# A two-layer hybrid transformer backbone: the additions and multiplications of GpSimd go to VectorE

## The chip, the cores and the metric

The kernel runs on one core of one Trainium2 chip. The metric is the device time of one execution in microseconds (us), from start to end. Three runs of the kernel before took 3027.81, 3032.04 and 3037.07 us; the median is 3032.04 us. A further execution was taken by the hardware profiler and took 3032.16 us.

A core has a TensorE (PE, matrix products; PEld is its weight load), a VectorE (DVE), a ScalarE (ACT), a GpSimd (POOL) and a SyncE (SP), which issues the DMAs here. Each engine takes its own instructions strictly in the order in which they stand in its queue and waits for the others by semaphores.

## The reference

Two layers over 1024 latent tokens and 256 context tokens of width 1024, all in float32. Each layer is a token mixer followed by a SwiGLU channel mixer:

```python
h = rms_norm(x, g_norm1[l]) * (1.0 + sc1) + sh1
mix, mix_c = token_mixers(h, hc, ...)        # h @ w_in, then three groups of heads:
    # A: attention over a window of +-128 tokens and the context, QK-norm, rotary positions
    # B: real part of a 2-D DFT and a linear map
    # C: chunked gated linear attention (GLA), forward and backward
x = x + gt1 * (mix @ w_out[l])
h2 = rms_norm(x, g_norm2[l]) * (1.0 + sc2) + sh2
x = x + gt2 * swiglu(h2, w_ffn_in[l], w_ffn_out[l])   # hidden width 2816 = 22 tiles of 128
```

The scales and shifts (sc, sh, gt) come from `silu(c) @ w_mod[l] + b_mod[l]`. In the first layer the context stream goes through the same steps; the second layer only reads it.

## The kernel before, in words

All activations lie with features on the partitions and tokens along the row. Every float32 operand of a large product is split in two: `hi` is the operand rounded to the fast matmul format (ACT, line 163), `lo` is what is left (`raw - hi`, DVE, line 164). A product then takes three matmuls of 128x128 by 128x512 (lines 168 to 170). So each weight tile and each activation tile passes once through ACT and once through DVE before PE can use it.

A layer has these stages, which overlap at their ends. Times are those of the profiled execution.

- **Mixing stage** (up to about 900 us in layer 0, 1730 to 2300 us in layer 1): projections (`project`, `qk`), attention (`attend`), GLA (`gla`), the Fourier mixer, and in layer 0 the whole context FFN, woven together by a table of weights (`weave`). `qk` rotates q and k: DVE shuffles, one engine multiplies the shuffled copy by the sines (line 597), DVE multiplies the other by the cosines (598) and adds (599). `gla` masks a 256-wide block of scores in two directions with `copy_predicated` into the two halves of one buffer `abuf` (DVE, 874) and adds the two halves (876); the next block overwrites the buffer, so it waits for that addition. Line 906 multiplies the normed GLA output by the gate.
- **Output projection, norm and the first FFN tiles** (`lat_proj`, `norm_raw`, `ffn_plain`).
- **The loop of seven products** (`ffn_seven`, about 1034 to 1425 us in layer 0 with 20 of the 22 hidden tiles, about 2505 to 2755 us in layer 1 with 14). For the latent tokens the gate and up products of a hidden tile are a Strassen-Winograd scheme: instead of eight half-depth products it does seven (`p` 0 to 6), 12 matmuls each. Five of the seven weights are sums or differences of halves of the gate and up tiles (line 1222), made three products ahead of their use. The activation side needs sums and differences as well: `combos1` makes `1+` (additions) and `4-`, `3-` (subtractions, all in `combo`, line 1156), `combos2` makes `7+` and adds `r += x` in place for `6+` (line 1164). Each of these tiles is then split (163, 164). The results of the products are joined by DVE from PSUM (lines 1270 to 1286), and a PSUM bank is used again once it has been read: the first product's bank (p 0) is read by an ACT copy (1268) and used again by p 3; the second product's (p 1) is read by the DVE addition 1270 and used again by p 4. In layer 0 two modulation rows of the next layer are made per hidden tile: a DMA of one row of `wmodT` and a DVE multiply-and-reduce (328), which stands in DVE's queue and waits there for its DMA.
- **Down projection** (`down_tiles`, `down_mm`).

The order within an engine's queue is not the order of the code: the tile framework's scheduler sets it from the priorities of the code's order, its own idea of when an operand is ready, and the buffers that come free. Another engine for an instruction therefore changes the order of others too.

Of the kernel before, what the change touches and what calls it, by code (L numbers as in the profile page):

```python
# [13 lines left out]
ALU = mybir.AluOpType  # L14
# [30 lines left out]
class Prog:  # L45
# [539 lines left out]
    def qk(self, l, s, nm, j, ps, t0, n, rope):  # L585
        nc, mp = self.nc, self.mp
        raw, sq, a = self.ptmp(n, t0)
        nc.scalar.copy(raw, ps)
        nc.scalar.activation(sq, ps, ACTF.Square)
        ms = self.t_ps(n)  # L590
        nc.tensor.matmul(ms, self.onesbd[:], sq, start=True, stop=True)
        nr = self.neg_rstd(ms, 64.0, sq, a)
        g = self.nqkg[:, l, 0:1] if nm == "q" else self.nqkg[:, l, 1:2]
        nc.vector.scalar_tensor_tensor(raw, raw, g, nr, ALU.mult, ALU.mult)
        if rope is not None:
            nc.vector.stream_shuffle(sq, raw, mask=[(i + 16) % 32 for i in range(32)])
            nc.gpsimd.tensor_tensor(sq, sq, rope[:, 1, :], ALU.mult)
            nc.vector.tensor_tensor(raw, raw, rope[:, 0, :], ALU.mult)
            nc.vector.tensor_tensor(raw, raw, sq, ALU.add)
        hi, lo = sq.bitcast(F32R), raw.bitcast(F32R)  # L600
        self.split(raw, hi, lo)
        if nm == "q":
            dst = self.dram[s, "q"]
            b0, b1 = t0 // 128, (t0 + n) // 128
            for half in range(2):
                h = half * 4 + j
                for part, src in ((0, hi), (1, lo)):
                    nc.sync.dma_start(
                        dst[b0:b1, part * 64:part * 64 + 64, h, :].rearrange("b p q -> p b q"),
                        src[half * 64:half * 64 + 64, :].bitcast(F32).rearrange("p (b q) -> p b q", q=128))  # L610
        else:
            kd = self.kdl if s == "l" else self.kdc
            for kv in range(2):
                for half, src in ((0, hi), (1, lo)):
                    nc.sync.dma_start(
                        kd[half * 64:half * 64 + 64, kv, t0:t0 + n].bitcast(F32), src[kv * 64:kv * 64 + 64, :].bitcast(F32))
# [105 lines left out]
    def gla(self, l, s, need):  # L722
# [34 lines left out]
        for j in range(2):  # L757
# [99 lines left out]
            for c in range(nq):  # L857
                cs = slice(c * cw, (c + 1) * cw)
                yield from self.wait((l, s, "gr", j, (c + 1) * cw))
                ats = []  # L860
                for hh in range(2):
                    qd, en, st, _ = heads[hh]
                    tps = []
                    for d in range(2):
                        tp = self.g_ps(cw)
                        rows = slice(d * 64, d * 64 + 64)
                        for b in range(cw // 128):
                            bs = slice(c * cw + b * 128, c * cw + (b + 1) * 128)
                            nc.tensor.matmul(tp[:, b * 128:(b + 1) * 128], en[rows, bs], qd[rows, bs], start=True, stop=True)
                        tps.append(tp)  # L870
                    at = tmp("e")
                    for z in range(0, cw, 256):
                        for d in range(2):
                            nc.vector.copy_predicated(
                                self.abuf[d], self.glam[d][:].rearrange("p a b -> p (a b)"), tps[d][:, z:z + 256])
                        nc.gpsimd.tensor_tensor(at[:, z:z + 256], self.abuf[0], self.abuf[1], ALU.add)
                    ats.append(at)
                    yield 2.0
                O = self.g_ps(cw)
                for hh in range(2):  # L880
                    h = 2 * j + hh
                    qd, en, st, _ = heads[hh]
                    at = ats[hh]
                    orow = slice(hh * 64, hh * 64 + 64)
                    for b in range(cw // 128):
                        gb = c * (cw // 128) + b
                        nc.tensor.matmul(O[orow, b * 128:(b + 1) * 128], vg[:, gb, 128 + h * 64:192 + h * 64],
                                         at[:, b * 128:(b + 1) * 128], start=True, stop=False)
                        for z in range(2):
                            ch = 2 * gb + z  # L890
                            nc.tensor.matmul(O[orow, b * 128 + z * 64:b * 128 + z * 64 + 64],
                                             st[:, ch::nch], qd[:, ch * 64:(ch + 1) * 64],
                                             start=False, stop=z == 1)
                ob = tmp("b")
                sq = tmp("kt")
                nc.scalar.copy(ob, O)
                nc.scalar.activation(sq, O, ACTF.Square)
                yield 4.0
                ms = self.g_ps(cw)
                nc.tensor.matmul(ms, self.onesbd[:], sq, start=True, stop=True)  # L900
                a = tmp("e")
                nr = self.neg_rstd(ms, 64.0, sq, a)
                nc.vector.scalar_tensor_tensor(ob, ob, self.nglg[:, l:l + 1], nr, ALU.mult, ALU.mult)
                sr = tmp("e")
                nc.sync.dma_start(sr, self.dram[s, "sr"][j, :, cs])
                nc.gpsimd.tensor_tensor(ob, ob, sr, ALU.mult)
                nc.sync.dma_start(self.dram[s, "mix"][:, 6 + j, cs], ob)
                yield 0.9
        self.emitted.add((l, s + "gla"))
# [241 lines left out]
    def combo(self, name, pool, tag, parts):  # L1151
        self.B[name] = self.half(pool, tag)
        for k in range(4):
            a, b, op = parts(k)
            t = self.t(self.tp, [128, 512], F32, "nx", 3)[:]
            (self.nc.vector if "+" in name else self.nc.gpsimd).tensor_tensor(t, a, b, op)
            self.split(t, *self.B[name](k))
            yield 1

    def combos2(self):  # L1160
        r, x = self.raw0, self.raw1
        yield from self.combo("7+", self.fp, FS, lambda k: (r(k + 4), x(k + 4), ALU.add))
        for k in range(4):
            self.nc.gpsimd.tensor_tensor(r(k), r(k), x(k), ALU.add)
            yield 1
        self.B["6+"] = self.half(self.fp, FS)
        for k in range(4):
            self.split(r(k), *self.B["6+"](k))
            yield 1
# [29 lines left out]
    def ffn_seven(self, l, fs, fps):  # L1199
# [7 lines left out]
        def weights(i):  # L1207
# [11 lines left out]
                    (g2, u2, ALU.subtract), (u1, g1, ALU.subtract)][p]  # L1219
            if isinstance(pair, tuple):  # L1220
                src = self.t(self.tp, [128, 512], F32, "c1", 2)[:]
                nc.gpsimd.tensor_tensor(src, *pair)  # L1222
            else:
                src = pair
            tag = (("wh", 3), ("wl", 3), ("HC", 4))[min(self.wslot % 10 % 3 if self.wslot % 10 < 9 else 2, 2)]
# [264 lines left out]
```

## Time and profile before

| | |
|---|---|
| median of three runs | 3032.04 us |
| profiled execution | 3032.16 us |
| its span (first to last instruction) | 3030.4 us |
| PE busy | 2810.1 us (93%) |
| DVE busy | 1925.5 us (64%) |
| ACT busy | 1362.1 us (45%) |
| POOL busy | 365.6 us (12%), 266 instructions |

"Busy" is the time in which an engine had an instruction in work. Matmuls overlap at their ends, and DVE's instructions by some tens of nanoseconds, so the time that one more instruction adds is read from start to start. PEclk is the granted clock of TensorE as a share of the full one (1.00 is 2.4 GHz, 0.50 is 1.2 GHz). The mean over the profiled execution was 0.959.

### The profile page before, as it was taken

The page shows a single profiled execution, that of the slowest core. Times are in us where ns is not written, and L with a number is a line of the kernel's source. Part 1 is how long each engine was busy: PE and PEld are TensorE (multiplying, and loading weights), DVE is VectorE, ACT ScalarE, POOL GpSimd, SP SyncE. Part 2 cuts the span into 40 slices and gives each one's busy share as a digit, 9 for nine tenths or more (in the row PEclk, how much of TensorE's full clock was granted, in tenths as well). Part 3 has the DMA queues.
Part 4 walks back from the last instruction along what each step waited for, and adds up shares of the span by engine and source line. Part 5 has one row for each costly group of instructions (what it writes and reads, how often), then busy time and mean ns, then how long its engine had stood idle before and what let it go on. Part 6 is the DMA issues. An engine that isn't in the chain of part 4 may idle for free. (4 is left out here: it accounts for less than half of the span.)

```text
span 3030.4 us, 38144 instructions
## 1 busy us (share of the span) xinstructions
PE 2810.1 (93%) x14042; PEld 2248.4 (74%) x14042; DVE 1925.5 (64%) x3041; ACT 1362.1 (45%) x2476; POOL 365.6 (12%) x266
## 2 busy tenths in 40 slices
PE   6999997979989889999999898996898999999999
PEld 3577676868888677887877776664676887888887
DVE  4266677787675877777547468685675567555332
ACT  3356565565554533333324356554445454333321
POOL 0000100000000434332000000010100014331000
PEclk9999997989999999999999999996899999999999
DMA  7754452434555244444746534334244332224542
GB/s 250 257 159 132 127 156 72 144 94 138 178 185 180 84 165 134 141 135 145 257 160 214 190 112 141 114 94 139 86 127 152 125 126 94 84 84 136 201 157 94
DMA packets 198042, 436.45 MB, mean 144 GB/s; under 512 B 23712, under 2 KB 59296, under 8 KB 196832
## 3 DMA queue, kind: packets, MB, share of 16 engines
q1 hardware_dynamic: 197856, 434.03, 44.1%
q8 instruction: 110, 1.80, 0.2%
q14 instruction: 76, 0.62, 0.1%
HBM read 361.85 MB, written 69.48 MB: 142 GB/s over the span
## 5 line engine op out<-in xcount | busy, mean ns | idle before, releaser
L164 DVE TENSOR_TENSOR wl<-raw,wh 128x1024 fp32r<-128x1024 f32 (+1 forms) x310 | 377.4, 1220 | 365.2 <-ACT wh L163 345.3
L163 ACT CAST wh<-raw 128x1024 fp32r<-128x1024 f32 (+2 forms) x319 | 325.7, 1025 | 528.2 <-PE mm L169 194.6
L168 PE MATMUL mm<-H,wh 128*128 128x512 f32 x716 | 290.4, 408 | 4.1 <-ACT H L163 3.7
L170 PE MATMUL mm<-H,wl 128*128 128x512 f32 x728 | 290.7, 401 | 0.0
L169 PE MATMUL mm<-H,wh 128*128 128x512 f32 x716 | 287.9, 404 | 0.8 <-DVE H L164 0.8
L168 PE MATMUL mm<-F,wh 128*128 128x512 f32 x536 | 210.4, 392 | 6.6 <-ACT F L163 3.9
L169 PE MATMUL mm<-F,wh 128*128 128x512 f32 x536 | 210.6, 393 | 0.7 <-DVE F L164 0.7
L170 PE MATMUL mm<-F,wl 128*128 128x512 f32 x524 | 205.7, 393 | 0.5 <-DVE wl L164 0.5
L168 PE MATMUL f<-F,wh 128*128 128x512 f32 x444 | 174.0, 392 | 13.8 <-ACT GC L1268 12.3
L170 PE MATMUL f<-F,wl 128*128 128x512 f32 x456 | 177.5, 390 | 0.4 <-DVE wl L164 0.4
L169 PE MATMUL f<-F,wh 128*128 128x512 f32 x444 | 173.4, 391 | 0.0
L168 PEld LDWEIGHTS mm<-H,wh 128*128 128x128 f32 x716 | 136.3, 191 | 37.1 <-issue 5.8
L168 PE MATMUL mm<-HC,wh 128*128 128x256 f32 x544 | 160.0, 295 | 3.2 <-ACT HC L163 1.8
L170 PEld LDWEIGHTS mm<-H,wl 128*128 128x128 f32 x728 | 138.4, 190 | 30.2 <-issue 2.7
L169 PEld LDWEIGHTS mm<-H,wh 128*128 128x128 f32 x716 | 136.6, 191 | 29.8 <-issue 1.9
L169 PE MATMUL mm<-HC,wh 128*128 128x256 f32 x544 | 157.2, 290 | 0.6 <-DVE HC L411 0.3
L170 PE MATMUL mm<-HC,wl 128*128 128x256 f32 x544 | 155.4, 287 | 0.8 <-DVE wl L164 0.8
L328 DVE CUSTOM_DVE_ANT_0 na<-raw,GC 128x1024 bf16<-128x1024 f32 x64 | 90.0, 1406 | 88.9 <-DMA raw<-wmodT 84.9
L674 ACT ACTIVATE P<-S,nm 128x640 f32<-128x640 f32 (+2 forms) x144 | 104.6, 732 | 71.4 <-DVE nm L670 70.7
L168 PEld LDWEIGHTS mm<-F,wh 128*128 128x128 f32 x536 | 101.1, 189 | 30.5 <-ACT F L163 5.5
L668 DVE TENSOR_REDUCE mx<-S 128x2 f32<-128x1280 f32 (+2 forms) x68 | 95.6, 1406 | 40.9 <-PE S L663 40.4
L696 PE MATMUL t<-ident,P 128*128 128x128 f32 x640 | 110.5, 289 | 11.6 <-DVE pt L701 4.3
(592 smaller groups left out, 6989.7 us busy)
## 6 DMA issues: line engine op xcount, KB each, us to landing
raw<-wff SPq DMA_DIRECT2D x228, 512.0 KB, 3.8
raw<-wmodT SPq DMA_DIRECT2D x64, 512.0 KB, 4.1
raw<-wfm SPq DMA_DIRECT2D x52, 512.0 KB, 4.0
nx<-gd SPq DMA_DIRECT2D x88, 256.0 KB, 3.8
raw<-wout SPq DMA_DIRECT2D x40, 512.0 KB, 3.7
XC<-wff SPq DMA_DIRECT2D x34, 512.0 KB, 3.8
pt<-wmod SPq DMA_DIRECT2D x64, 256.0 KB, 4.5
qld<-q_l SPq DMA_DIRECT2D x64, 256.0 KB, 4.2
```

The source lines that it names most:

```text
L163: self.nc.scalar.copy(hi, raw)
L164: (eng or self.nc.vector).tensor_tensor(lo, raw, hi.bitcast(F32), ALU.subtract)
L168: mm(ps, wh, xh, start=start, stop=False, skip_group_check=skip)
L169: mm(ps, wh, xl, start=False, stop=False, skip_group_check=skip)
L170: mm(ps, wl, xh, start=False, stop=stop, skip_group_check=skip)
L328: self.nc.vector.tensor_tensor_reduce(out=junk[:], in0=raw, in1=cs[s][:], op0=ALU.mult, op1=ALU.add, scale=1.0, scalar=0.0, accum_out=self ...
L668: nc.vector.tensor_reduce(mx[:, :nh], st[:, c0:c0 + nh * n].rearrange("p (a n) -> p a n", n=n), axis=AX.X, op=ALU.max)
L674: nc.scalar.activation(P[:, :n], st[:, c0 + z * n:c0 + (z + 1) * n], ACTF.Exp, bias=nm[:, hh:hh + 1], accum_out=sums[:, hh:hh + 1])
L696: nc.tensor.transpose(tp[:, hh * 128:(hh + 1) * 128], P[:, c:c + 128], self.ident[:])
```

## The change

Every `tensor_tensor` that was issued on GpSimd is issued on VectorE. Nothing else is edited. POOL keeps only its memsets.

```diff
@@ qk
-            nc.gpsimd.tensor_tensor(sq, sq, rope[:, 1, :], ALU.mult)
+            nc.vector.tensor_tensor(sq, sq, rope[:, 1, :], ALU.mult)
@@ gla
-                        nc.gpsimd.tensor_tensor(at[:, z:z + 256], self.abuf[0], self.abuf[1], ALU.add)
+                        nc.vector.tensor_tensor(at[:, z:z + 256], self.abuf[0], self.abuf[1], ALU.add)
...
-                nc.gpsimd.tensor_tensor(ob, ob, sr, ALU.mult)
+                nc.vector.tensor_tensor(ob, ob, sr, ALU.mult)
@@ combo
-            (self.nc.vector if "+" in name else self.nc.gpsimd).tensor_tensor(t, a, b, op)
+            self.nc.vector.tensor_tensor(t, a, b, op)
@@ combos2
-            self.nc.gpsimd.tensor_tensor(r(k), r(k), x(k), ALU.add)
+            self.nc.vector.tensor_tensor(r(k), r(k), x(k), ALU.add)
@@ ffn_seven, weights
-                nc.gpsimd.tensor_tensor(src, *pair)
+                nc.vector.tensor_tensor(src, *pair)
```

The scheduler lays the queues out anew. Two places at the start of the loop of seven products in layer 0 show it. ACT's queue before, around the copy of the first product's bank (L1268). `nx` are the differences of activations (line 1156) and `c1` the sums of weights (line 1222), both made by POOL; `H` and `F` are split activations, `wh`, `wl` and `HC` split weights, `f` and `mm` PSUM banks:

```order
L163 CAST H_1662_9498<-nx_1666_9502 128x512
L576 ACTIVATE nx_1659_9485<-nx_1659_9485 128x512
L163 CAST wh_1704_9657<-c1_1703_9655 128x512
L163 CAST wl_1706_9682<-c1_1705_9680 128x512
L163 CAST H_1662_9498<-nx_1667_9506 128x512
L163 CAST H_1663_9499<-nx_1669_9537 128x512
L1268 COPY GC_1671_9546<-f_1681_9567 128x512
L163 CAST wh_1716_9740<-XC_1696_9626 128x512
```

The same place of ACT's queue after:

```order
L163 CAST F_1646_9433<-nx_1661_9494 128x512
L163 CAST wl_1693_9603<-raw_1673_9548 128x512
L576 ACTIVATE nx_1659_9485<-nx_1659_9485 128x512
L1268 COPY GC_1671_9546<-f_1681_9567 128x512
L163 CAST H_1662_9498<-nx_1666_9502 128x512
L163 CAST H_1662_9498<-nx_1667_9506 128x512
L163 CAST H_1663_9499<-nx_1669_9537 128x512
L163 CAST H_1663_9499<-nx_1670_9541 128x512
```

The copy L1268 has moved ahead of the casts of all four `H` tiles; before, three of them and two casts of weight sums stood ahead of it. Second place, DVE's queue before, up to the addition L1270 that frees the second product's bank:

```order
L164 TENSOR_TENSOR H_1665_9501<-nx_1669_9537,H_1663_9499 128x512
L164 TENSOR_TENSOR wl_1706_9682<-c1_1705_9680,wl_1706_9682 128x512
L1156 TENSOR_TENSOR nx_1690_9578<-XA_60_382,F_1486_8446 128x512
L164 TENSOR_TENSOR H_1665_9501<-nx_1670_9541,H_1663_9499 128x512
L1156 TENSOR_TENSOR nx_1691_9582<-XA_60_382,F_1486_8446 128x512
L164 TENSOR_TENSOR F_1688_9576<-nx_1690_9578,F_1686_9574 128x512
L1156 TENSOR_TENSOR nx_1692_9586<-XA_60_382,F_1487_8447 128x512
L164 TENSOR_TENSOR F_1688_9576<-nx_1691_9582,F_1686_9574 128x512
L1156 TENSOR_TENSOR nx_1694_9606<-XA_60_382,F_1487_8447 128x512
L164 TENSOR_TENSOR F_1689_9577<-nx_1692_9586,F_1687_9575 128x512
L1270 TENSOR_TENSOR GC_1671_9546<-GC_1671_9546,f_1682_9568 128x512
```

DVE's queue after, up to the same addition:

```order
L1164 TENSOR_TENSOR XA_60_382<-XA_60_382,F_1484_8444 128x512
L164 TENSOR_TENSOR H_1665_9501<-nx_1669_9537,H_1663_9499 128x512
L164 TENSOR_TENSOR H_1665_9501<-nx_1670_9541,H_1663_9499 128x512
L1156 TENSOR_TENSOR nx_1690_9578<-XA_60_382,F_1486_8446 128x512
L1156 TENSOR_TENSOR nx_1691_9582<-XA_60_382,F_1486_8446 128x512
L1156 TENSOR_TENSOR nx_1692_9586<-XA_60_382,F_1487_8447 128x512
L164 TENSOR_TENSOR F_1688_9576<-nx_1690_9578,F_1686_9574 128x512
L164 TENSOR_TENSOR F_1688_9576<-nx_1691_9582,F_1686_9574 128x512
L164 TENSOR_TENSOR F_1689_9577<-nx_1692_9586,F_1687_9575 128x512
L1156 TENSOR_TENSOR nx_1694_9606<-XA_60_382,F_1487_8447 128x512
L1164 TENSOR_TENSOR XA_60_382<-XA_60_382,F_1484_8444 128x512
L1270 TENSOR_TENSOR GC_1671_9546<-GC_1671_9546,f_1682_9568 128x512
```

The splits of weight sums (`wl_1706`) have moved behind L1270, and the in-place sums L1164 and the differences of `3-` and `4-` now stand ahead of it. Counted from the split of the last weight tile of the stage before (`wl_1657`), 31 instructions stand between the two in DVE's queue before, and 40 after.

## Rows read from the trace of the kernel before

**Rows 1.** Page: busy time, share of the span, instructions of each engine.

```profile
PE 2810.1 (93%) x14042; PEld 2248.4 (74%) x14042; DVE 1925.5 (64%) x3041; ACT 1362.1 (45%) x2476; POOL 365.6 (12%) x266
```

**Rows 2.** Stretches: length; busy time and instructions by engine; PEclk, DMA share, GB/s.

```profile
500.00:900.00 400.00, 365.40 (x2652) 318.17 (x2651) 301.85 (x570) 217.30 (x432) 22.10 (x20) 0.96 0.44 139
1800.00:2200.00 400.00, 335.37 (x1764) 250.97 (x1762) 285.66 (x500) 209.00 (x414) 33.83 (x29) 0.88 0.38 116
1100.00:1400.00 300.00, 293.46 (x1270) 240.03 (x1269) 238.79 (x306) 101.86 (x177) 114.89 (x80) 0.99 0.43 143
2500.00:2750.00 250.00, 245.08 (x1077) 201.62 (x1077) 147.83 (x210) 93.57 (x162) 102.80 (x70) 1.00 0.25 85
1042.00:1062.00 20.00, 5.00 (x14) 3.40 (x12) 19.73 (x19) 9.70 (x18) 13.84 (x9) 0.70 0.20 66
1062.00:1082.00 20.00, 19.46 (x77) 15.88 (x78) 15.23 (x27) 10.63 (x21) 5.47 (x3) 0.88 0.39 125
1202.00:1422.00 220.00, 219.59 (x968) 181.17 (x967) 176.00 (x226) 70.79 (x127) 78.36 (x58) 1.00 0.43 140
```

**Rows 3.** Groups of POOL: count, busy us, mean ns, idle before and its releasers.

```profile
L1222 POOL TENSOR_TENSOR c<-raw,XC 128x512 f32<-128x512 f32 x68 | 97.4, 1432 | 87.9 <-DVE HC L164 34.4 <-DVE wh L164 32.1 <-DVE wl L164 19.0
L876 POOL TENSOR_TENSOR nx<-XA 128x256 f32<-128x256 f32 x36 | 32.5, 902 | 488.8 <-DVE XA L874 282.8 <-DVE es L680 195.1 <-DVE es L678 7.0
L597 POOL TENSOR_TENSOR P<-P,XC 128x512 f32<-128x512 f32 x10 | 15.9, 1592 | 433.8 <-ACT HC L829 163.5 <-DVE P L596 148.2 <-DVE mod_0l L305 110.8
L1164 POOL TENSOR_TENSOR XA<-XA,F 128x512 f32<-128x512 f32 x8 | 11.9, 1482 | 0.5
```

**Rows 4.** Groups of DVE in the loop, 1100 to 1400 us.

```profile
L328 DVE CUSTOM_DVE_ANT_0 na<-raw,GC 128x1024 bf16<-128x1024 f32 x34 | 51.4, 1512 | 41.1 <-DMA raw<-wmodT 41.0
L1282 DVE TENSOR_TENSOR XA<-XA 128x512 f32<-128x512 f32 x15 | 21.6, 1443 | 1.6 <-ACT XA L1281 0.7
L1280 DVE TENSOR_TENSOR XA<-f,XA 128x512 f32<-128x512 f32 x8 | 5.4, 680 | 0.7 <-PE f L170 0.7
```

**Rows 5.** Groups of DVE where POOL has no arithmetic, 1450 to 1700 us.

```profile
L328 DVE CUSTOM_DVE_ANT_0 na<-raw,GC 128x1024 bf16<-128x1024 f32 x22 | 26.9, 1223 | 35.4 <-DMA raw<-wmodT 35.4
L164 DVE TENSOR_TENSOR F<-nx,F 128x512 fp32r<-128x512 f32 x38 | 25.4, 687 | 12.3 <-ACT F L163 11.9
L1282 DVE TENSOR_TENSOR XA<-XA 128x512 f32<-128x512 f32 x1 | 0.7, 684 | 0.0
```

**Rows 6.** Stretch, line 164 on DVE alone: length, busy time and count.

```profile
1100.00:1400.00 300.00, 106.52 (x110) 0.99 0.43 143
```

**Rows 7.** Order of time, DVE: start, duration, instruction, idle before it.

```profile
1022.05 1.22 DVE L164 TENSOR_TENSOR wl<-raw,wh 128x1024 fp32r<-128x1024 f32 x1
1031.47 1.78 DVE L164 TENSOR_TENSOR wl<-c,wl 128x512 fp32r<-128x512 f32 x1
1058.20 0.68 DVE L1156 TENSOR_TENSOR nx<-XA,F 128x512 f32<-128x512 f32 x1
1058.80 0.68 DVE L164 TENSOR_TENSOR F<-nx,F 128x512 fp32r<-128x512 f32 x1
1061.81 0.67 DVE L1270 TENSOR_TENSOR GC<-GC,f 128x512 f32<-128x512 f32 x1
```

**Rows 8.** Order of time, ACT, before the copy of the first product's bank.

```profile
1046.24 0.62 ACT L163 CAST H<-nx 128x512 fp32r<-128x512 f32 x1 [3.27 <-POOL nx L1156]
1052.08 0.62 ACT L163 CAST H<-nx 128x512 fp32r<-128x512 f32 x1 [1.05 <-POOL nx L1156]
1052.60 0.58 ACT L1268 COPY GC<-f 128x512 f32<-128x512 f32 x1
```

**Rows 9.** Order of time, PE: the two waits at the loop's start.

```profile
1041.97 0.39 PE L170 MATMUL f<-F,HC 128*128 128x512 f32 x1
1053.24 0.80 PE L168 MATMUL f<-F,wh 128*128 128x512 f32 x1 [10.88 <-ACT GC L1268]
1062.54 0.80 PE L168 MATMUL f<-H,wl 128*128 128x512 f32 x1 [4.66 <-DVE GC L1270]
```

**Rows 10.** Line 874 on DVE: idle before it until the named releaser, us, times.

```profile
  POOL nx L876: 6.7, 11
```

## The prediction

> **What bounds the kernel now.** I read the busy times first. PE is busy 93% of the span, DVE 64%, POOL 12% [rows 1], so only what lets PE wait can move the time, and a busier DVE costs nothing until PE waits for it. The stretches come next, because the shares differ by stage [rows 2]. In the loop of seven products PE works without a gap once it runs: 219.6 of 220 us in layer 0, 245.1 of 250 in layer 1. In the mixing stages it idles, 34.6 of 400 us at 500 to 900 and 64.6 of 400 at 1800 to 2200, with DVE at 75% and 71% and POOL nearly idle (22 and 34 us). POOL's work sits in the two loops. DVE there is busy 239 of 300 us in layer 0, and 41 us of its 61 idle us are waits of the modulation rows for their DMA [rows 4]. So layer 0's loop is where DVE has least room: some 20 us in 300.
>
> One thing in the trace says that POOL's work is not free for DVE. The same subtraction or multiplication on DVE is longer where POOL works beside it: L1282, two operands in SBUF, means 1443 ns in the loop of layer 0 and 684 where POOL has nothing to do; the modulation row takes 1512 against 1223 [rows 4, 5]; the splits of line 164 take 106.5 us for 110 in the loop, 968 each, against 687 [rows 5, 6]. L1280 has one operand in PSUM and stays at 680 [rows 4]. So an instruction of POOL holds up a DVE instruction that reads SBUF twice.
>
> The Trainium skill states it as a rule (SBUF — State Buffer, "SBUF: two separate sides"): VectorE and GpSimd share one pair of ports, and an operation of VectorE with two SBUF inputs and one of GpSimd that reads SBUF exclude each other for a whole instruction, whoever starts first. The rows above agree (1443 against 684, and 680 for the one with a PSUM input). If the two merely shared the bandwidth, some relief would come too, so the sum below does not hang on it.
>
> **What the change removes and adds.** POOL's 260 arithmetic instructions go: 170 of line 1222 (the row shown, with x68, and three like it with 34 each), 36 of L876, 20 of L597, 16 of L1156, 8 of L1164 and 10 of L906 [rows 3]. They took 900 to 1590 ns on POOL. On DVE the same subtraction L1156 is 0.68 us long, and the next instruction starts 0.60 us after it [rows 7], so I take 0.60 us for 512 columns and a little over half, 0.35, for the 38 of 256 columns.
>
> In 1100 to 1400 us DVE gets 79 additions of line 1222: 47.4 us. It is relieved of the waits for POOL: 110 x (968 - 687) = 30.9 us on line 164, 15 x (1443 - 684) = 11.4 on L1282, 34 x (1512 - 1223) = 9.8 on L328, together 52 us. So DVE's load in this stretch does not grow; it falls by about 5 us. That is the first half of the forecast: the loop stays PE's. Cost there 0; if the relief fails, see the rival below.
>
> The Trainium skill has a rule that speaks against more DVE instructions (VectorE: DVE Perf Modes, "The DRAIN you can't avoid"): after each operation the pipe empties before the next begins, so what counts is the number of operations. The trace shows starts 0.60 us apart for durations of 0.68 [rows 7], so part of that is overlapped here. By the rule an added operation would cost the whole 0.68, the load in the stretch above would be 54 us against 52 of relief, and the restart below would come 40 x 0.08 = 3.2 us later, a time of about 3023. I go by the starts.
>
> **The start of the loop in layer 0.** This is where PE pays for POOL. After the third product PE stops at 1042.0, starts p 3 at 1053.24 after 10.88 us, and after it waits 4.66 us more for p 4 [rows 9]. The first wait ends with ACT's copy L1268, which frees a PSUM bank. That copy's input, the first product, was there before the third had ended; it stood in ACT's queue behind casts that waited for POOL's differences, the last until 1052.1 [rows 8]. The second ends with DVE's L1270 at 1061.81, which stood at the end of a convoy: DVE and POOL alternated, and DVE's 512-column instructions took 1.78 us instead of 0.68 [rows 7]. 31 instructions lie between `wl<-raw,wh` (1022.05) and L1270 (1061.81): 38.6 us after the first had its 1.1 us, 1.25 each.
>
> Afterwards there are 40 between the two, with no POOL: 40 x 0.60 = 24 us, and L1270 at 1022.1 + 1.1 + 24 = 1047.2. Beside it the casts on ACT (0.62 us each [rows 8], about one for two of DVE's) keep up, and L1268 stands ahead of the four H casts in the new order. So p 3 follows at 1042.2 with no wait and ends 12 x 0.227 = 2.7 us later (0.227 = 219.59 / 968 [rows 2]), and p 4 starts at 1047.2 to 1049: a wait of 2.3 to 4. I take 4 instead of 15.5: **-11.5 us**. Bounds: -15.5 if none is left, -4 if DVE waits for ACT at every second split (the 31 instructions' average of 1.25 us would again come near).
>
> The clock: in 1042 to 1082 it was granted at 0.70 and 0.88 after the long wait, and 91 matmuls took 24.5 us [rows 2]; at 0.227 they take 20.6. That is 3.9 us, kept wholly or in part if a wait of 4 us no longer brings it down. I take half, **-2**; bounds 0 and -4.
>
> What is late next: PE arrives 13 us earlier at products whose weights DVE must still add and split, and these splits now stand behind L1270. Before, 300 - 293.5 = 6.5 us of waits followed in 1100 to 1400 [rows 2]. Each new addition also stands behind modulation rows that wait 41.1/34 = 1.2 us on average for their DMA. The cover is the lead of three products, 8 us. I add **+3**; bounds 0 and +10.
>
> **Layer 1's loop.** DVE gets 70 instructions there, 42 us on 148 of 250 [rows 2]: 76%, hidden. Of PE's 4.9 us of waits I credit **-1** (bounds -4, +3).
>
> **The mixing stages.** L597 and L598 ran side by side on paper only: both read SBUF twice, L597 took 1.59 us, and two on DVE take 1.2. L876 cost the next masking 6.7 us of waits in 11 places [rows 10], which go, for 36 x 0.35 = 13 us of work. In 500 to 900 and 1800 to 2200 the 49 instructions of POOL become some 25 us on DVE's 301.9 and 285.7 of 400 [rows 2], against relief of the same kind as above, which I put at half to all of it. Net near nothing, but the scheduler has laid out the queues of all engines anew from the first q tile on, and among 99 us of PE's waits a few may grow or go. **-1**, bounds -12 and +10.
>
> **Sum.** -11.5 - 2 + 3 - 1 - 1 = -12.5 us on the profiled 3032.16, which is the median of the runs (3032.04) to 0.1 us. Predicted: **3020 us**, its own range 3008 to 3027.
>
> **Rivals.** *Nothing that can be measured, 3030 us.* PE's earlier restart is given back within the loop: DVE stays the slower in the catch-up, where each product needs some six DVE instructions, 3.6 us, against PE's 2.7, and the waits behind the restart grow by what was saved. For it: DVE has only 20 us of true idle time in 300 there. Against it: from 1202 on PE has no waits, and DVE's load is not greater than before.
>
> *DVE becomes the bound of layer 0's loop, 3067 us.* One queue then holds the additions, the splits, the joins and the modulation rows with their DMA waits. If the relief does not come, DVE needs 238.8 + 41 + 47.4 = 327 us per 300, 9% more, over the loop's 390 us: +35 us. It decides from the point where less than 27 of the 52 us of relief arrive (238.8 + 41 + 47.4 - 27 = 300). For it: the addition of a weight, which ran on POOL while DVE waited for a modulation row, now waits behind it. Against it: the durations in rows 4 to 6 show the relief itself, instruction by instruction.
>
> *More than forecast, 3003 us.* The clock stays up at the restart, no wait is left there (-19.4), and of the 99 us of waits in the two mixing stretches a tenth (-9.9) goes with the shorter chains. For it: the waits of L874 for L876 and the slow L597 [rows 3, 10]. Against it: POOL did little there.
>
> **How the numbers follow.** The forecast has a chance of 0.47, no visible change 0.28, the DVE bound 0.13, the larger gain 0.12. A measurement of this kernel can tell about 0.3%, 9 us, from no change. Faster by more, below 3023: 0.85 of the forecast (0.40), the larger gain (0.12) and a little of the second (0.01): 0.53. Slower by more, above 3041: most of the DVE bound (0.12) and a tenth of the second case (0.03), 0.15. The rest, 0.32, is within. The range reaches from 3002, just past the larger gain, to 3046, where a part of the DVE bound is taken in.
>
> **What would show it.** After: PE's waits at L1268 and L1270 at the loop's start in layer 0 together under 6 us; DVE's 512-column instructions all near 0.68 us; L1282 near 684 and L328 near 1223 ns in the loop; DVE busy 230 to 245 of 300 us there though it holds 79 instructions more; PE at 99% from 1200 on. Wrong would be: PE waiting for line 164 or 1222 in every hidden tile of layer 0 (the DVE bound), L1282 still above 1 us without POOL, or changes of more than 10 us in the mixing stages.

## The result

The changed kernel took 2993.79 us in the median of four runs (2991.63 to 3001.51), beside 3033.78 us for the kernel before in four runs on the same chip. The medians differ by 40.0 us; the ratio is 0.9875, with a 95% interval of 0.9851 to 0.9899, which is some 38 us of the time before. The forecast was 3020 us, in a range of 3002 to 3046. The direction was right, and the gain is three times the forecast and lies outside the range.

The page's first part, after, beside [rows 1]: DVE has 260 instructions more and is busy 30 us longer, and POOL keeps six memsets.

```profile
PE 2803.1 (93%) x14042; PEld 2250.1 (75%) x14042; DVE 1955.1 (65%) x3301; ACT 1364.8 (45%) x2476; POOL 1.3 (0%) x6
```

Shares over the whole span don't show where the time went. The two loops of seven products do, cut from PE's first matmul of the loop to the start of DVE's last join. The kernel before, layer 0 and layer 1, in the columns of [rows 2]:

```profile
1034.00:1459.00 425.00, 398.38 (x1704) 324.56 (x1704) 338.24 (x434) 155.11 (x269) 154.65 (x106) 0.97 0.43 141
2514.30:2790.00 275.70, 270.78 (x1191) 222.87 (x1190) 163.59 (x234) 103.25 (x176) 96.96 (x66) 1.00 0.27 92
```

The same two after, and then the stretches of [rows 2]:

```profile
1040.60:1433.30 392.70, 388.59 (x1705) 320.62 (x1704) 326.74 (x536) 152.84 (x260) 0.00 (x0) 1.00 0.47 152
2489.80:2759.30 269.50, 269.50 (x1190) 223.23 (x1190) 192.50 (x293) 101.63 (x172) 0.00 (x0) 1.00 0.28 95
...
500.00:900.00 400.00, 362.63 (x2594) 318.33 (x2595) 295.10 (x566) 214.23 (x427) 0.00 (x0) 0.93 0.43 135
1800.00:2200.00 400.00, 337.48 (x1812) 251.05 (x1811) 284.82 (x528) 203.93 (x403) 0.00 (x0) 0.89 0.40 119
1100.00:1400.00 300.00, 300.00 (x1325) 248.47 (x1324) 247.40 (x405) 107.61 (x182) 0.00 (x0) 1.00 0.46 149
2500.00:2750.00 250.00, 250.00 (x1104) 207.07 (x1104) 174.71 (x266) 89.09 (x150) 0.00 (x0) 1.00 0.26 89
```

The same matmuls of layer 0's loop (1704 and 1705 in the records) take 392.7 us instead of 425.0 (-32.3), and those of layer 1 take 269.5 instead of 275.7 (-6.2). Together that is -38.5 us, about the whole change. From 1100 to 1400 and in all of layer 1's loop PE has no idle time left. The rest of the program did not get shorter: the part between the loops takes 1056.5 us (1055.3 before), the last stage 240.4 in both, and the part ahead of the first loop 1040.6 (1034.0 before). That last number changes from one execution to the next, also with the same kernel (further executions of the changed one began the loop at 1036.2 and 1034.7 us), and the profiled execution of 3001.51 us is the longest of the four.

At the start of layer 0's loop, after. In order of time, first DVE, then ACT, then PE (start, duration, instruction, idle before it), beside [rows 7 to 9]:

```profile
1028.56 1.22 DVE L164 TENSOR_TENSOR wl<-raw,wh 128x1024 fp32r<-128x1024 f32 x1
...
1053.78 0.67 DVE L1270 TENSOR_TENSOR GC<-GC,f 128x512 f32<-128x512 f32 x1
```

```profile
1043.47 0.59 ACT L1268 COPY GC<-f 128x512 f32<-128x512 f32 x1 [1.59 <-PE f L170]
```

```profile
1054.59 0.76 PE L168 MATMUL f<-H,wl 128*128 128x512 f32 x1 [3.00 <-ACT F L163]
```

ACT now copies the first product's bank as soon as that product is done (it waits for PE), so p 3 starts without a gap. One wait is left, 3.00 us ahead of p 4. The row names a cast of ACT, which ended at 54.50; L1270 ended at 54.45, so which of the two released it can't be told from the row. 10.88 + 4.66 us became 3.00.

DVE's groups in the loop, 1100 to 1400 us, after, beside [rows 4]:

```profile
L328 DVE CUSTOM_DVE_ANT_0 na<-raw,GC 128x1024 bf16<-128x1024 f32 x36 | 44.0, 1222 | 16.8 <-DMA raw<-wmodT 16.5
L1282 DVE TENSOR_TENSOR XA<-XA 128x512 f32<-128x512 f32 x16 | 11.0, 685 | 0.7 <-ACT XA L1281 0.7
L1280 DVE TENSOR_TENSOR XA<-f,XA 128x512 f32<-128x512 f32 x8 | 5.5, 686 | 0.7 <-PE f L170 0.7
```

Line 164 on DVE alone in the same stretch (length, busy time and count, PEclk, DMA share, GB/s), beside [rows 6]:

```profile
1100.00:1400.00 300.00, 77.41 (x114) 1.00 0.46 149
```

The three kinds of DVE instruction that were long before are now as short as in [rows 5]: L1282, L328 and line 164 take 685, 1222 and 679 ns (77.41 / 114), where they took 1443, 1512 and 968.

What the forecast had let stand shows in PE's groups behind the start, 1080 to 1440 us (mean of one, then idle before them and its releasers). Before:

```profile
L168 PE MATMUL f<-F,HC 128*128 128x512 f32 x74 | 29.5, 399 | 2.2 <-ACT HC L163 2.0 <-ACT XA L1268 0.2
...
L168 PE MATMUL mm<-F,wl 128*128 128x512 f32 x32 | 13.1, 408 | 3.6 <-ACT XA L1268 3.6
...
L168 PE MATMUL f<-H,wh 128*128 128x512 f32 x28 | 11.7, 419 | 3.1 <-DVE XA L1270 3.1
```

After, the largest wait of the same view:

```profile
L168 PE MATMUL f<-F,HC 128*128 128x512 f32 x72 | 28.1, 391 | 0.8 <-ACT HC L163 0.8
```

Before, these and smaller ones came to 11 us. After, they come to 1.1 us. The waits before were of two kinds. 5.0 us ended with a join or split of DVE (1.2 of them behind a modulation row that waited for its DMA). The longest of these, 2.1 us, shows the usual case: the join L1270 is short itself, but stood behind two splits of 1.78 and 1.74 us, where a split alone takes 0.69 [rows 5].

```profile
1187.82 1.78 DVE L164 TENSOR_TENSOR wl<-c,wl 128x512 fp32r<-128x512 f32 x1
...
1190.66 1.74 DVE L164 TENSOR_TENSOR HC<-XC,HC 128x512 fp32r<-128x512 f32 x1
1192.33 0.67 DVE L1270 TENSOR_TENSOR XA<-XA,f 128x512 f32<-128x512 f32 x1
```

The others, 5.8 us, ended with ACT. The longest wait of all, 3.6 us, is one of them: the copy L1268 stood in ACT's queue behind casts of weight sums that had not yet come from POOL. The first of the waits (2.0 us, at 1096.84) ended with the cast of a sum ahead of which POOL had itself waited for the DMA of its weights.

```profile
1124.54 0.62 ACT L163 CAST HC<-c 128x512 fp32r<-128x512 f32 x1 [3.13 <-POOL c L1222]
1126.20 0.62 ACT L163 CAST wh<-c 128x512 fp32r<-128x512 f32 x1 [1.05 <-POOL c L1222]
1126.73 0.58 ACT L1268 COPY XA<-mm 128x512 f32<-128x512 f32 x1
```

### The profile page after: what moved, and what is told of

It is laid out like the page before. It is cut to its first block, busy times and chain, and to the rows that moved or that the text cites. A ratio compares the mean times of both kernels' runs of the same rounds, so it can differ in the third digit from the quotient of the medians.

```text
span 2999.7 us, 37870 instructions
## 1 busy us (share of the span) xinstructions
PE 2803.1 (93%) x14042; PEld 2250.1 (75%) x14042; DVE 1955.1 (65%) x3301; ACT 1364.8 (45%) x2476; POOL 1.3 (0%) x6
## 4 chain that ended last, share of the span: by engine, by line
PE 71%; DVE 11%; DMA 8%; ACT 6%; issue 3%; SPq 1%; ACTq 0%; DVEq 0%
PE mm L168 11%; PE mm L169 11%; PE mm L170 11%; PE f L170 5%; PE f L168 5%; PE f L169 5%; DMA raw<-wff 3%; PE t L709 2%; PE t L696 2%; PE t L168 2%; PE t L169 2%; PE t L170 2%; DVE wl L164 2%; ACT wh L163 1%; PE S L652 1%
## 5 line engine op out<-in xcount | busy, mean ns | idle before, releaser
L168 PEld LDWEIGHTS mm<-F,wh 128*128 128x128 f32 x536 | 101.0, 188 | 31.2 <-ACT F L163 6.2
L696 PE MATMUL t<-ident,P 128*128 128x128 f32 x640 | 112.0, 292 | 12.2 <-DVE P L689 4.7
L169 PEld LDWEIGHTS mm<-F,wh 128*128 128x128 f32 x536 | 101.1, 189 | 22.7 <-DVE F L164 1.5
```

The source lines that it names most:

```text
L168: mm(ps, wh, xh, start=start, stop=False, skip_group_check=skip)
L169: mm(ps, wh, xl, start=False, stop=False, skip_group_check=skip)
L696: nc.tensor.transpose(tp[:, hh * 128:(hh + 1) * 128], P[:, c:c + 128], self.ident[:])
```

## The experiments

Two theories were open once the result was known. **Lock:** POOL's reads of SBUF stretch DVE's instructions, the joins and splits among them for which PE waits; without them all waits go. **Handoff:** what costs is that a weight sum passes from DVE's queue to POOL's and back (POOL waits for a buffer, DVE for the sum); on one engine the passing is gone. Beside them stood **order**: only the new order at the loop's start counts. "Loop" below is layer 0's, cut as above. The runs were made on several chips, on which the kernel before took 3024.5 to 3033.8 us, so each ratio is against the kernel before on the same chip, and the ranges in microseconds are to be read with that in mind.

**1. The weight sums alone on DVE**, the rest as before.

```diff
@@ ffn_seven, weights (kernel before)
-                nc.gpsimd.tensor_tensor(src, *pair)
+                nc.vector.tensor_tensor(src, *pair)
```

> Only the weight sums (line 1222, 170 of the 260 instructions) go to VectorE; the activation sums and differences stay on GpSimd. Lock theory (a GpSimd instruction that reads SBUF holds up VectorE instructions with two SBUF inputs): the steady loop of layer 0 gains (L1282 near 684 ns, L328 near 1223 from 1100 to 1400 us), the start of the loop keeps most of its convoy, so a part of the gain: 3005 to 3020 us. Order theory (the gain came from the new queue order at the loop's start, the copy L1268 ahead of the casts): near the kernel before, 3025 to 3035. Handoff theory (a weight sum on GpSimd is slow to come, and PE waits for it): most of the gain, 2995 to 3005.

3000.97 us, ratio 0.9899 [0.9883, 0.9916]. Its loop's stretch, then PE at its start in order of time:

```profile
1038.10:1438.80 400.70, 390.53 (x1704) 321.40 (x1703) 331.71 (x532) 157.21 (x268) 10.13 (x7) 0.99 0.44 149
```

```profile
1047.79 0.79 PE L170 MATMUL f<-F,HC 128*128 128x512 f32 x1 [3.61 <-DVE HC L164]
...
1053.12 0.50 PE L168 MATMUL f<-F,wh 128*128 128x512 f32 x1 [1.18 <-ACT GC L1268]
...
1060.47 0.50 PE L168 MATMUL f<-H,wl 128*128 128x512 f32 x1 [4.33 <-DVE GC L1270]
```

The time lies below the lock theory's range and inside the handoff theory's, so by the time alone this run speaks for handoff; the order theory is out. The trace is as the lock theory had it: L1282 takes 687 ns and L328 1224. The loop is 24.3 us shorter although 9.1 us of waits stay at its start. The waits at the start fall by 6.4 us, those behind it from 11.1 to 1.1, and the rest is faster matmuls: the sums bring most of the gain. One step, the sums on DVE, took away both the stretched splits and POOL's late sums, so this run can't tell the two theories apart.

**2. The activation sums alone on DVE.**

```diff
@@ combo, combos2 (kernel before)
-            (self.nc.vector if "+" in name else self.nc.gpsimd).tensor_tensor(t, a, b, op)
+            self.nc.vector.tensor_tensor(t, a, b, op)
...
-            self.nc.gpsimd.tensor_tensor(r(k), r(k), x(k), ALU.add)
+            self.nc.vector.tensor_tensor(r(k), r(k), x(k), ALU.add)
```

> Only the activation sums and differences of the loop (lines 1156 and 1164, 24 instructions) go to VectorE; the weight sums stay on GpSimd. Lock theory: the long waits at the start of layer 0's loop (15.5 us) shrink to some 6, the later ones and L1282 at 1443 ns stay: 3010 to 3022 us. Order theory: nearly the whole gain, 2995 to 3005. Handoff theory of the weight sums: 3020 to 3030.

3014.79 us, ratio 0.9943 [0.9924, 0.9961]. Its loop, a group of DVE (1100 to 1400 us), and two of PE over the loop:

```profile
1030.80:1445.20 414.40, 395.38 (x1701) 322.40 (x1700) 334.56 (x442) 151.65 (x262) 138.88 (x96) 0.98 0.43 144
```

```profile
L1282 DVE TENSOR_TENSOR XA<-XA 128x512 f32<-128x512 f32 x15 | 22.8, 1520 | 1.6 <-ACT XA L1281 0.7
```

```profile
L168 PE MATMUL f<-F,HC 128*128 128x512 f32 x84 | 33.7, 401 | 5.0 <-ACT HC L163 4.8 <-ACT XA L1268 0.2
...
L168 PE MATMUL f<-H,wh 128*128 128x512 f32 x32 | 13.4, 420 | 5.3 <-DVE XA L1270 5.3
```

The time is in the lock theory's range and outside the two others. This is the mirror image of number 1. The waits at the start fall from 15.5 to 3.3 us, L1282 stays long at 1520 ns, and the waits behind the start do not merely stay: they grow from 11.1 to 15.7 us (414.40 - 395.38 = 19.0 in the loop, less 3.3), which fits PE's earlier arrival. The loop gets 10.6 us shorter, close to what the forecast had for the restart. The two parts come to 24.3 + 10.6 = 34.9 us beside the change's 32.3, so they add up nearly. The new order at the start can explain a third of the gain at most, since this run also took POOL's differences and in-place sums away from there.

**3. The mixing stages alone on DVE** (lines 597, 876 and 906), **and the loops alone** (lines 1222, 1156 and 1164).

```diff
@@ qk, gla (kernel before; the second kernel is the changed one with these three lines put back)
-            nc.gpsimd.tensor_tensor(sq, sq, rope[:, 1, :], ALU.mult)
+            nc.vector.tensor_tensor(sq, sq, rope[:, 1, :], ALU.mult)
...
-                        nc.gpsimd.tensor_tensor(at[:, z:z + 256], self.abuf[0], self.abuf[1], ALU.add)
+                        nc.vector.tensor_tensor(at[:, z:z + 256], self.abuf[0], self.abuf[1], ALU.add)
...
-                nc.gpsimd.tensor_tensor(ob, ob, sr, ALU.mult)
+                nc.vector.tensor_tensor(ob, ob, sr, ALU.mult)
```

> Only the instructions of the mixing stages (lines 597, 876, 906, 66 of 260) go to VectorE. All theories: within 6 us of the kernel before, 3028 to 3040 us, with both loops as before; a gain of 10 us or more would say that the mixing stages had a part in it.

> The instructions of the loops (lines 1222, 1156, 1164, 194 of 260) go to VectorE; those of the mixing stages stay on GpSimd. Lock theory: the whole gain, 2990 to 3000 us. If the mixing stages had a part, 3003 or more.

The mixing stages alone: 3029.25 us, 1.0003 [0.9992, 1.0013]. The loops alone: 2990.36 us, 0.9871 [0.9855, 0.9888], with a loop of 392.7 us. Both times are in their ranges. On the chip of numbers 4, 5 and 7 the changed kernel ran once more:

> The changed kernel once more, for comparison on the same chip and for a second profile: 2990 to 3002 us. If the stages before layer 0's loop are 6 us longer than before in the first profile by chance, they are not so here; if the new order makes them so, they are.

2994.52 us, 0.9903 [0.9887, 0.992]; its layer 0 loop began at 1036.2 us, so most of the first profile's delay ahead of the loop was chance. The whole gain is the loops'; 66 instructions more or less on DVE in the mixing stages can't be told from nothing.

**4. POOL reads beside DVE, and nobody waits for it.** The changed kernel, in which POOL makes each weight sum as well (504 of its columns), into a tile `padr` that nothing reads. The line that gives this tile its name is left out of the diff here and in number 6.

```diff
@@ ffn_seven, weights (changed kernel)
                 nc.vector.tensor_tensor(src, *pair)
+                nc.gpsimd.tensor_tensor(self.padr[:], pair[0][:, 0:504], pair[1][:, 0:504], pair[2])
```

> The changed kernel with 170 idle additions on GpSimd: beside each weight sum of VectorE, GpSimd adds the same two operands (504 columns) into a pad that nobody reads. No engine waits for a result of GpSimd. Lock theory: L1282 above 1000 ns again, VectorE's load in layer 0's loop past what the loop holds, 3015 to 3050 us. Handoff theory (what cost was the way over the slow engine) and order theory: 2992 to 3002, as the changed kernel.

3066.91 us, 1.0134 [1.0119, 1.0149]: slower than the kernel before, and more than the lock theory's range had it. Its loop, two groups of DVE, and PE's waits in 1100 to 1400 us (in all, times, longest; lines 1271 and 1287 here are 1270 and 1286 before):

```profile
1036.20:1485.90 449.70, 408.40 (x1705) 328.75 (x1704) 405.74 (x546) 155.52 (x269) 146.72 (x92) 0.96 0.40 133
```

```profile
L164 DVE TENSOR_TENSOR HC<-c,HC 128x512 fp32r<-128x512 f32 x28 | 23.7, 846 | 0.0
...
L1287 DVE TENSOR_TENSOR XA<-XA 128x512 f32<-128x512 f32 x13 | 17.5, 1345 | 0.0
```

```profile
PE f L168 <- DVE XA L1271: 13.5, 5, 4.3
PE t L168 <- DVE XA L1271: 7.0, 4, 2.4
```

Nothing waits for POOL's result, and still the join of line 1286, which takes 684 ns in the changed kernel, takes 1345, DVE is busy 405.7 us of the loop instead of 326.7 for ten instructions more, and PE waits for DVE's joins. POOL does hold the weight buffers until it has read them here, which number 6 takes away. In this run DVE has the additions and the stretching together; in the kernel before it had only the stretching.

**5. POOL in the chain, and reads nothing.** The changed kernel with two memsets by POOL of the sum's tile ahead of each sum: DVE has to wait for POOL, POOL for DVE's buffer.

```diff
@@ ffn_seven, weights (changed kernel)
                 src = self.t(self.tp, [128, 512], F32, "c1", 2)[:]
+                nc.gpsimd.memset(src, 0.0)
+                nc.gpsimd.memset(src, 0.0)
                 nc.vector.tensor_tensor(src, *pair)
```

> The changed kernel with GpSimd in the chain of each weight sum and reading nothing: GpSimd writes zeros twice into the tile (0.53 us each) before VectorE overwrites it with the sum, so that VectorE waits for GpSimd as it did for the casts before. Lock theory with a lock only against instructions of GpSimd that read: VectorE's durations stay near 0.68 us, and the time within 10 us of the changed kernel, 2992 to 3004. Handoff theory: most of the gain is lost, 3015 to 3035.

2995.79 us, 0.9901 [0.9886, 0.9916], as the changed kernel and as the lock theory had it. Its loop, then a group of DVE in 1100 to 1400 us (line 1284 here is 1282 before):

```profile
1036.90:1430.20 393.30, 389.19 (x1706) 320.68 (x1706) 325.62 (x535) 152.61 (x259) 100.96 (x193) 1.00 0.46 152
```

```profile
L1284 DVE TENSOR_TENSOR XA<-XA 128x512 f32<-128x512 f32 x16 | 10.9, 684 | 0.7 <-ACT XA L1283 0.7
```

POOL is busy 101 us of the loop, is passed every tile, and costs 0.6 us. So the passing by itself costs nothing, and the handoff theory falls in that form. What this run does not have is a sum that is made on POOL: POOL can clear its tile early, and DVE waited for it only 3.0 us in 1100 to 1400. The waits for late sums on ACT, seen before, are not imitated here.

**6. POOL reads only its own tile.** As number 5 with one memset, after which POOL reads one column of the sum's tile and adds its own tile of 504 columns to itself. The own tile is cleared once when the kernel starts, in a line left out here.

```diff
@@ ffn_seven, weights (changed kernel)
                 src = self.t(self.tp, [128, 512], F32, "c1", 2)[:]
+                nc.gpsimd.memset(src, 0.0)
+                nc.gpsimd.tensor_tensor(self.padr[:, 0:1], src[:, 0:1], src[:, 0:1], ALU.add)
+                nc.gpsimd.tensor_tensor(self.padr[:], self.padr[:], self.padr[:], ALU.add)
                 nc.vector.tensor_tensor(src, *pair)
```

> The changed kernel with GpSimd reading SBUF beside the weight sums, tied to no operand of the loop: per weight sum GpSimd clears the tile (as in the run with the cleared tile, which cost nothing), reads one column of it, and then adds a pad of 504 columns to itself, a pad that no other engine touches. Unlike in the run with the idle additions, no weight buffer is held longer by it. Lock theory: VectorE's subtractions and joins with two SBUF inputs are long again, and the loop of layer 0 takes 425 to 455 us instead of 393: 3020 to 3070 us. If the idle additions cost time only because they held the weight buffers: within 8 us of the changed kernel, 2990 to 3004.

3044.45 us, 1.0055 [1.0037, 1.0072], in the lock theory's range. Its loop, groups of DVE in 1100 to 1400 us (lines 165 and 1279 are 164 and 1275 before), and what DVE waited for POOL there:

```profile
1036.40:1469.30 432.90, 399.66 (x1698) 323.28 (x1697) 370.26 (x535) 151.38 (x259) 219.60 (x291) 0.98 0.40 137
```

```profile
L165 DVE TENSOR_TENSOR wl<-c,wl 128x512 fp32r<-128x512 f32 x24 | 23.4, 974 | 0.0
...
L1279 DVE TENSOR_TENSOR XA<-XA 128x512 f32<-128x512 f32 x14 | 12.1, 864 | 0.0
```

```profile
DVE c L1226 <- POOL padr L1224: 11.7, 15, 1.7
```

No weight buffer is tied to POOL now, and the loop is 40.2 us longer than the changed kernel's; DVE is busy 370.3 us for 535 instructions, where it was 326.7 for 536. Those 43.5 us are stretched instructions. A smaller part is waiting: the sums waited 11.7 us for POOL's one-column read in 300 us. Number 4 has the stretching without any such wait, number 5 the passing without the stretching. So POOL's additions, which read SBUF, stretch DVE's instructions and cost PE time, and its memsets, which don't read, do not. That it is the read, and not something else in which an addition differs from a memset, was not tested by itself, nor why number 4 is still 17 us slower in the loop than this one.

The Trainium skill (SBUF — State Buffer, "SBUF: two separate sides") says that a VectorE operation with two SBUF inputs is blocked only by a GpSimd operation that reads SBUF. Numbers 5 and 6 agree: beside memsets the join of line 1275, with two SBUF inputs, takes 686 ns, and beside an addition of a tile that has nothing to do with it 864; the join of line 1282 rises less, from 684 to 740.

**7. A longer lead.** The kernel before, with weight sums made four products ahead instead of three.

```diff
-        ahead = 3
+        ahead = 4
```

> The kernel before with the weights of the loop made four products ahead instead of three. Handoff theory: the longer lead covers GpSimd's slow sums, and the later waits go (6.5 us in 1100 to 1400): 3015 to 3026 us. Lock theory: VectorE is held up just as much, within 6 us of the kernel before, 3027 to 3040.

3024.82 us, 0.9997 [0.9985, 1.0009]; the loop takes 425.5 us, against 425.0. The time lies in the handoff theory's range only because the kernel before, too, took no more than 3024.53 us on this chip. The later waits did not go as that theory had it (9.6 us idle in 1100 to 1400, 6.5 before). But the run decides little, because the sums hardly came earlier. The same sum of POOL, in the kernel before and here:

```profile
1109.40 1.29 POOL L1222 TENSOR_TENSOR c<-raw 128x512 f32<-128x512 f32 x1 [3.79 <-DVE mod_1c L328]
1104.92 1.28 POOL L1222 TENSOR_TENSOR c<-raw 128x512 f32<-128x512 f32 x1 [3.71 <-DVE mod_1c L328]
```

That is 75.4 and 74.3 us behind the loop's first matmul: 1.1 us earlier, less than one product of 2.7 us. What a sum that really comes earlier would be worth stays untested.

**8. The last wait at the start.** The changed kernel with two steps of the activation sums per product instead of three, which leaves 29 instead of 40 instructions ahead of L1270; then the same with the mixing stages on POOL; and the changed kernel a third time, on the same chip as the latter.

```diff
@@ ffn_seven (changed kernel)
-            for _ in range(3):
+            for _ in range(2):
                 next(sums, None)
```

> The changed kernel with two instead of three steps of the last activation sums taken per product at the start of the loop, so that 29 instead of 40 instructions stand between the last split and the addition that frees the second bank. That addition comes 11 x 0.60 = 6.6 us earlier, and the last wait of 3.0 us at the loop's start and its half-speed stretch of 3.4 us go: 2986 to 2995 us, some 4 us under the changed kernel. If the sums that are put off are then late for the sixth and seventh products, as before or slower.

> The loops' instructions on VectorE, those of the mixing stages left on GpSimd, and two steps of the activation sums per product. If the two edits that each measured some 4 us under the changed kernel are real and add up: 2985 to 2990 us and 4 to 9 us under the changed kernel run beside it. If they were scatter of the stages before the loop: within 3 us of it.

> The changed kernel beside it on the same chip: 2990 to 2998 us.

2989.7 us, 0.987 [0.9847, 0.9894]; 2986.76 us, 0.9868 [0.985, 0.9886]; and the changed kernel itself 2988.73 us, 0.9879 [0.9857, 0.9902]. The wait of 3.00 us goes, and smaller ones come in its place, as this row of PE in the first of the three shows:

```profile
1049.75 0.50 PE L168 MATMUL mm<-H,HC 128*128 128x512 f32 x1 [1.15 <-ACT HC L163]
```

The loops take 391.6, 390.0 and 392.7 us. No changed kernel ran on the chip of the first. The two edits together were 2.0 us under the changed kernel beside them, within the 3 us that had been named as scatter, and that kernel itself came out 1.3 us under its range. A gain of 1 to 3 us may be there, but the runs can't tell it from none, so none of these is a better version.

## Why the prediction was right in direction and wrong in size

Layer 0's loop lost 32.3 us. PE's idle time in it went from 425.0 - 398.4 = 26.6 us to 392.7 - 388.6 = 4.1 us, so 22.5 of the 32.3 are idle time, and the other 9.8 are matmuls that took less time, most of it a matter of the clock, as shown below.

- **The restart (-11.5): right.** The waits went from 15.5 to 3.0 us; forecast were 2.3 to 4. L1270 was put at 24 us behind the end of the last `wl` split, 40 instructions at 0.60 us from start to start: 1028.56 + 1.1 + 24 = 1053.7, measured 1053.78. By the whole durations of 0.68 it would have come 3 us later. Number 2, which changes little but the start, took 12.2 us off the waits there.
- **"What is late next" (+3): wrong, and this is the step that failed.** The term asked only what arrives late once PE comes earlier. It took the waits behind the start, 6.5 us idle in [rows 2] at 1100 to 1400, as a stock that could only grow (bounds 0 and +10), and the relief of DVE was booked as load alone: 47 us of additions against 52 us of relief, "Cost there 0". The load did stay: 238.8 us for 1270 matmuls before, 247.4 for 1325 after, 0.188 and 0.187 us each. But the waits, 11 us over the whole loop, were no matter of load. They stood behind single stretched splits and behind POOL's late sums, and both went with POOL's work: about -10 in place of +3. Number 2 shows where the step's reasoning would have held: with the weight sums still on POOL, PE's earlier arrival made these waits grow by 4.6 us. With the sums on DVE (number 1) they fell to 1.1. How the 10 us divide between the stretching and the late sums stays open, since no run has the late sums without the stretching, and the runs that stretch without them (numbers 4 and 6) load DVE with the sums besides.
- **The clock (-2): right for its stretch, but 9.8 in all.** The step looked at one stretch, 1042 to 1082, where by its count 3.9 us were lost; 1.3 are left after (25 matmuls in 7.00 us in the row below, 5.7 at 0.227). The clock also fell behind the three longest of the later waits, which the step did not price. Before, the three stretches with these waits (columns as above):

```profile
1094.00:1104.00 10.00, 7.61 (x26) 5.50 (x25) 8.32 (x10) 3.48 (x6) 5.50 (x5) 0.83 0.39 109
...
1124.00:1134.00 10.00, 6.52 (x20) 4.77 (x21) 9.05 (x9) 4.39 (x8) 5.64 (x4) 0.83 0.51 169
...
1184.00:1204.00 20.00, 17.70 (x70) 13.82 (x69) 17.17 (x22) 7.07 (x12) 10.81 (x7) 0.91 0.55 176
```

  PE idled 2.4, 3.5 and 2.3 us in them. The granted clock was 0.83 in the first two: a third of the time at the lower of its two levels, 1.2 GHz, the rest at 2.4. The 116 matmuls of the three took 31.8 us, where they take 26.3 at 0.227. The short waits at 1425 to 1430 (1.0 and 1.2 us) and those in layer 1's loop left the clock at 1.00. After, one stretch of the loop is left with less than 1.00, around the wait of 3.00 us:

```profile
1050.00:1060.00 10.00, 7.00 (x25) 5.36 (x24) 9.86 (x17) 7.22 (x13) 0.00 (x0) 0.83 0.20 55
```

  So the waits that went cost 22.5 us as idle time and up to 9.8 more in slow matmuls behind them, of which these stretches show about 8. That the slow matmuls follow the waits is read from the traces; the clock was not varied by itself.
- **Layer 1's loop (-1): too small.** It lost 6.2 us and all of its idle time (4.9 us before, of which 2.8 ended with ACT's copy L1268 and 2.2 with DVE's join L1270). Number 1 shows the same loop at 269.2 us and number 2 at 271.4, so here either half of the change takes most of the waits away; which mechanism did it was not separated.
- **The mixing stages (-1): right.** Number 3 measured 1.0003.
- **The rivals.** DVE as the bound fell with L1282 at 685 ns: all of the relief arrived. Number 4 shows what it would have looked like, with the additions on DVE and part of the relief missing: 42 us above the kernel before on its chip, where the rival had 35. That its 3066.9 us look like the 3067 worked out is chance, since the chips differ, and only 24.7 of the 42 us are in layer 0's loop, where the rival had all of its 35. "Nothing that can be measured" fell with the waits behind the start. "More than forecast", 3003 us, came nearest in time, but it looked for the rest in the mixing stages, where there was none, so that a part of its nearness is luck.
- **The signs.** Four of five came true: 3.0 us of waits at the start, the short instructions, L1282 and L328, and PE without idle time from 1200 on. DVE was busy 247.4 us of the 300, a little over the 230 to 245 named, in a stretch that now holds 55 matmuls more. One reading of the prediction was off without effect on the sum: POOL's groups took up to 1716 ns each (line 1222, `c<-XC,raw`), not 1590.

What stays open: how the gain behind the start divides between stretched DVE instructions and late sums of POOL, why number 4 is slower than number 6, and why DVE's waits of the modulation rows for their DMA fell from 41.1 us [rows 4] to 16.8 in the same stretch. The last may be no more than where the idle time is booked; no run was made for that one.

## What to carry to other kernels

Where instructions of VectorE with two SBUF operands come out longer beside GpSimd's than alone, moving GpSimd's arithmetic over may cost VectorE little, as it did here, and the gain is not the saved load but the waits of the bound engine: sum every one of them in that stage, and ask of each whether its releaser was stretched, stood behind a stretched instruction, or waited for GpSimd. Don't carry such waits over as fixed when the change removes what they wait for. Add to the longer ones what the granted clock loses behind them. Before putting work on an idle GpSimd, compare the duration of VectorE's own instructions with and without it.

## What the runs showed of the hardware that was not expected

- Additions of GpSimd for whose results no engine waits made layer 0's loop 57 us longer (392.7 to 449.7, number 4). Additions on a tile of its own made it 40 us longer (432.9, number 6, where VectorE also waited for GpSimd's one-column reads, 11.7 us in 300); 193 memsets in the same place cost 0.6 us (393.3).
- VectorE's instructions of 512 columns kept starts 0.60 us apart for durations of 0.67 to 0.69 over a whole queue of 40.
- The stage ahead of the first loop ended between 1027.5 and 1040.6 us in executions, on several chips, of kernels that differ little or not at all there. Single differences of a few us between two traces mean nothing in it.
